# Residue-ordered keys, copied queries and negated scores in the dilated and windowed attention groups, with new durations for the planner

## The chip, the cores and the metric

One core of one Trainium2 chip runs the whole program. The metric is the device time of one execution in microseconds (us): 1769.04 us before, the median of three executions (1765.94, 1769.04, 1773.9). In this document PE is TensorE, DVE is VectorE, ACT is ScalarE, POOL is GpSimd, and SP is the engine that issues every DMA.

## The reference

The kernel computes one layer of a decoder trunk over 2048 tokens of width 1024. RMSNorm and one combined projection feed four groups of four heads; the merged heads are gated, projected by `w_out` and added to `x`:

```python
h = rms_norm(x, norm_w[layer]) @ w_in[layer]
o_a = dilated_attention(rms_norm(heads(a_q), g[0]), rms_norm(heads(a_k), g[1]), heads(a_v), tables[0])
o_b, _ = banded_attention(rms_norm(heads(b_q), g[2]), kb, vb, tables[1], SWA_WINDOW - 1, sink=attn_sinks[layer])
# group C: differential attention, group D: native sparse attention
y = jnp.concatenate([merge(o_a), merge(o_b), merge(o_c), merge(o_d)], axis=-1) * jax.nn.silu(silu_gate)
x = x + y @ w_out[layer]

DILATED_CONFIGS = ((128, 1), (512, 4), (2048, 16))
# dilated_attention: for each (window, rate) the tokens are folded into `rate` residue classes,
# banded_attention runs in each class over window // rate predecessors, and a softmax over the
# three log-sum-exps weighs the three outputs
# banded_attention: s = q k^T * 64**-0.5 + bias(dist * rate), invalid keys -1e30;
# m = max(s) (B: max with the sink); p = exp(s - m); o = p v / sum(p)
```

So a query block of 128 tokens of one residue class meets the 128 keys of its own block and, unless it is the first, the 128 of the block before it: 128 or 256 columns of scores. At rate 16 a class has one block, at rate 4 it has four, at rate 1 sixteen.

## The kernel before, in words

**Stages.** The projections of the groups run in the order C, D, A, B (`project`, one 512-column and one shorter accumulation for each of 16 row tiles and group). They are written as generators, "fillers", that hand PE work while attention waits. Attention runs group C, then D (window, compressed, selected), then A at rates 16 and 4 for each of its heads, then A at rate 1 in turns with B. The output projection (`out_proj`, matmuls on L2159) is the last filler: the half that needs C and D ("CD", reads `wb`) can run from the end of D on, the half that needs A and B ("AB", reads `keys`, `AQ`, `ow`) follows.

**What sets the order.** Nothing waits dynamically except on semaphores. While the program is built, a planner keeps an estimated clock for each engine (`T`), adds an estimated duration for each operation (`op("DVE", 72.0, e)`), and takes the next piece of PE work whose inputs should be there (`drive`, `fill_step`, `poll`, `defer`). The order in which instructions are written, on every engine and on SP's queue, comes from these estimates; a changed number can move instructions anywhere.

**Precision.** A float32 operand is split in a high and a low part of the type fp32r, each on its own rows; a score takes two matmuls (x = 0, 1) into one bank.

**Queries and keys.** `turn` in `project` transposes four 128-token tiles of normalised queries or keys (L741) into one bank; ACT and DVE scale and split them, and they are stored as [column of the head, token] in the DRAM tiles `TQ` and `TK`, tokens in natural order.

**A at rates 16 and 4** (`make_a`, `a_unit`): `ORDER` lists 32 units, for each head four of rate 16 and four of rate 4. `qk_load` brings one head's queries and keys into SBUF (`QK`; heads 0 and 2 lie in `wb`, heads 1 and 3 in `AQ` and `keys`). A unit has four blocks in two halves, in all eight score matmuls on L1646. A block of a residue class is addressed in place, with a step of `rate` elements, both as the weights and as the moving operand:

```python
return slice(c0, c0 + (n - 1) * r + 1, r)      # in cols(), used for Q and for K
```

At rate 16 all eight matmuls have 128 columns. At rate 4 two have 128 and six have 256; the first unit of rate 1 (contiguous operands, L1646 too) has the same eight.

After the matmuls DVE adds the bias and takes the maximum in one custom instruction for each block (L1651) followed by a read of its accumulator; a small instruction for each half (L1656) writes the negated maximum to column 65 of the output tile `AO`; ACT takes the exponential (L1662); PE transposes the weights (L393), ACT and DVE split them (L399, L403), PE multiplies by the values (L422), ACT evacuates (L371), PE transposes back (L435), and DVE sums the two halves (L439, or L442 on ACT and L444).

**Group B** does the same on L1948 to L1968, with a maximum against the sink (L1958) and a negation (L1959).

Of the kernel before, what the change touches and what calls it, by code (L numbers as in the profile page):

```python
# [22 lines left out]
NEG = -1e30  # L23
# [79 lines left out]
def tile_hybrid_heads(ctx, tc, a):  # L103
# [355 lines left out]
    expo = const.tile([128, 32], F32, name="expo")  # L459
# [8 lines left out]
    sink = const.tile([128, 4], F32, name="sink")  # L468
    nlam = const.tile([128, 1], F32, name="nlam")
# [38 lines left out]
    def small_constants(dl):  # L508
        V.tensor_scalar(gains[:, 0:1], gains[:, 0:1], 32.0 ** -0.5, None, op0=OP.mult)
        V.tensor_scalar(gains[:, 1:4], gains[:, 1:4], 0.125, None, op0=OP.mult)  # L510
# [6 lines left out]
        A.activation(ls[:, 2:4], ls[:, 0:2], AF.Exp)  # L517
        V.scalar_tensor_tensor(nlam, ls[:, 3:4], -0.2, ls[:, 2:3], op0=OP.add, op1=OP.subtract)


    def bias_vectors(bp):
# [4 lines left out]
        V.memset(tp[96:128, :], NEG)  # L526
# [65 lines left out]
    def weights(g, first=None):  # L592
# [21 lines left out]
        def split(i, rw, e):  # L614
# [4 lines left out]
            e = op("ACT", av(hi - lo, 1), e)  # L619
# [11 lines left out]
    def project(g, first=None):  # L631
# [26 lines left out]
        def evac_qk(t, ps, e, st, keep):  # L658
            run_chain()
            A.activation(st, ps, AF.Copy)  # L660
            e = op("ACT", av(512), e)
# [3 lines left out]
            e = op("ACT", av(nn), e)  # L665
# [5 lines left out]
            def two():  # L671
# [6 lines left out]
                e2 = op("DVE", 130.0)  # L678
                G.tensor_tensor(ss[:, :nh], ss[:, :nh], expo[:, :nh], op=OP.pow)  # L679
                e3 = op("POOL", 190.0 * nh + 100.0, e2)  # L680
# [55 lines left out]
        def turn(t3, j, gi, keep):  # L736
# [3 lines left out]
            for i in range(4):  # L740
                PE.transpose(ps[:, i * 128:(i + 1) * 128], keep[i][0][:, j * 128:(j + 1) * 128], ident)  # L741
# [194 lines left out]
    def row_steps(pool, store, qk, H, t, need, done):  # L936
# [5 lines left out]
        def chunk(ci, k0, n):  # L942
# [41 lines left out]
    def group_c():  # L984
      with tc.tile_pool(name="cs", bufs=1) as cs, tc.tile_pool(name="cw", bufs=2) as cw:
# [34 lines left out]
        def make(h, t0):  # L1020
# [66 lines left out]
            def close(ot):  # L1087
# [7 lines left out]
                def rest():  # L1095
                    for i in range(2):
                        A.activation(sq, O[:, i], AF.Square, accum_out=ss[:, i:i + 1])
                    e2 = op("ACT", 2 * av(64, 1), e)
# [4 lines left out]
                    e3 = op("POOL", 1966.0, e2)  # L1103
# [135 lines left out]
    def group_d():  # L1239
      with tc.tile_pool(name="dk", bufs=1) as dk:  # L1240
# [39 lines left out]
        def weigh(pool, ot, t, br, den, Y, first):  # L1280
# [5 lines left out]
            op("DVE", 557.0)  # L1286
# [8 lines left out]
        with tc.tile_pool(name="dq", bufs=1) as dq, tc.tile_pool(name="dw", bufs=2) as dw:  # L1295
# [19 lines left out]
            def win_unit(t):  # L1315
# [5 lines left out]
                def scores(h, c):  # L1321
# [51 lines left out]
        with tc.tile_pool(name="ds", bufs=1) as ds_:  # L1373
# [18 lines left out]
          with tc.tile_pool(name="dc", bufs=2) as dw:  # L1392
# [84 lines left out]
            def largest(t, n, selc, e):  # L1477
# [13 lines left out]
                e = op("DVE", 3412.0, e)  # L1491
# [84 lines left out]

    def qk_load(h, x):
# [5 lines left out]
        else:  # L1583
            c = slice((x - 2) // 2 * n, ((x - 2) // 2 + 1) * n)
            aready[h] = mv(raw(k)[x % 2::2, :, c], TK["A"][h * 64:h * 64 + 64, :, c])

# [29 lines left out]
    def group_ab():  # L1616
      with tc.tile_pool(name="aw", bufs=2) as aw, tc.tile_pool(name="as", bufs=1) as as_:
# [8 lines left out]


        def a_unit(r, q0, setup, room, need, source, stats, close):
# [5 lines left out]
            def scores(half):  # L1634
                qs, ks, H = source()
                if half == 0:
                    st["P"] = aw.tile([128, 4, 256], F32, name="ap", bufs=3)
                    st["mx"] = aw.tile([128, 4], F32, name="amx", bufs=4)
                P, mx, O = st["P"], st["mx"], stats()
# [17 lines left out]
                e = op("DVE", 72.0, e)  # L1657

                def weights():
                    for j in (2 * half, 2 * half + 1):  # L1660
                        n = 128 * (1 + prevs[j])
                        A.activation(P[:, j, :n], P[:, j, :n], AF.Exp, bias=O[:, j, 65:66], accum_out=O[:, j, 64:65])  # L1662
                        st["e"] = op("ACT", av(n, 2), e)
                    st["half"] = st.get("half", 0) + 1
                defer(e, weights)

# [22 lines left out]
        def make_a(n):  # L1689
# [8 lines left out]

            def setup():
                if h < 3 and 1 <= n % 8 <= 6:  # L1700
                    qk_load(h + 1, n % 8 - 1)
                if q0 == 0:
# [15 lines left out]
            def source():  # L1718
                Q, K = QK[h % 2]

                def cols(j, i0, n):
                    rho, i = divmod(q0 + j, nb)
                    c0 = rho + r * 128 * (i - i0)
                    return slice(c0, c0 + (n - 1) * r + 1, r)
                return (lambda j: Q[:, cols(j, 0, 128)]), (lambda x, j, p: K[:, x, cols(j, p, 128 * (1 + p))]), Hs[h, r]
# [62 lines left out]
            u = a_unit(r, q0, setup, room, lambda: max(at("s"), aready[h]), source,  # L1788
# [449 lines left out]
```

## Time and profile before

| | |
|---|---|
| median of three executions | 1769.04 us |
| the profiled execution's own time | 1773.27 us |
| its span, first to last instruction | 1771.5 us |
| granted PE clock, mean | 0.988 |
| PE busy | 1709.5 us (97%) |
| DVE, ACT, POOL busy | 76%, 61%, 39% |

The profile is one execution. A matmul's recorded end is modelled and matmuls overlap, so a busy PE can still do more in the same time: the distance between the starts of successive matmuls tells the pace, not the length of one. In the timeline, equal instructions that follow each other are merged into one row with their count.

### The profile page before, as it was taken

What the parts mean: (1) busy time and instruction counts of PE and PEld (TensorE: products, weight loads), DVE (VectorE), ACT (ScalarE), POOL (GpSimd) and SP (SyncE); (2) the same over time, 40 slices, a digit from 0 to 9 for tenths busy, and PEclk for the clock granted to TensorE, in tenths of its full rate; (3) what the DMA queues carried; (4) which work ended last, traced back from release to release, by engine and by line L of the source; (5) the groups of instructions that cost most, each with busy time, mean ns of one, the idle gap of its engine ahead of it and who ended that gap; (6) DMA issues with size and microseconds to landing.
All of it is one profiled execution on the core that took longest, in us unless ns stands there. A gap on an engine that the chain in (4) does not pass through costs nothing.

```text
span 1771.5 us, 31769 instructions
## 1 busy us (share of the span) xinstructions
PE 1709.5 (97%) x10035; PEld 1503.3 (85%) x10035; DVE 1338.3 (76%) x4072; ACT 1072.3 (61%) x2588; POOL 692.8 (39%) x841
## 2 busy tenths in 40 slices
PE   7999999999998999899999999999999999999999
PEld 5878878888887889788888889899979999789987
DVE  4446689898999998488747868888366876888873
ACT  4345466656776756467646656777356776576651
POOL 4567554544544554211255552222521112433331
PEclk9999999999999999899999999999999999999999
DMA  7763554444445424642367533232375778999986
GB/s 246 223 198 108 184 171 144 121 118 139 116 143 159 146 91 152 188 117 88 125 194 226 170 108 96 59 97 85 105 238 169 233 226 259 278 313 311 320 283 213
DMA packets 283480, 308.24 MB, mean 174 GB/s; under 512 B 80256, under 2 KB 201216, under 8 KB 282640
## 3 DMA queue, kind: packets, MB, share of 16 engines
q1 hardware_dynamic: 283312, 306.21, 55.8%
q8 instruction: 80, 1.31, 0.3%
q14 instruction: 88, 0.72, 0.1%
HBM read 219.47 MB, written 86.92 MB: 173 GB/s over the span
## 4 chain that ended last, share of the span: by engine, by line
PE 51%; DVE 3%; issue 1%; DMA 1%; ACT 1%; POOL 0%; SPq 0%; DVEq 0%; POOLq 0%
PE j L840 11%; PE j L2159 9%; PE o L422 9%; PE pt L393 8%; PE s L1646 4%; PE s L950 4%; PE pt L435 3%; PE s L1336 1%; PE pt L2123 1%; PE s L1948 1%; PE s L1435 1%; PE pt L741 0%; DVE pl L403 0%; PE j L1164 0%; DMA xt<-in_xt_dram 0%
## 5 line engine op out<-in xcount | busy, mean ns | idle before, releaser
L840 PE MATMUL j<-wb,xh 128*128 128x512 f32 (+2 forms) x2048 | 618.2, 382 | 18.8 <-DVE wb L622 9.6
L840 PEld LDWEIGHTS j<-wb,xh 128*128 128x128 f32 x2048 | 373.1, 190 | 67.4 <-DVE wb L622 14.5
L840 PE MATMUL j<-wb,xl 128*128 128x512 f32 (+2 forms) x1024 | 385.4, 376 | 0.6 <-POOL xl L577 0.6
L399 ACT ACTIVATE ph<-pt 128x512 fp32r<-128x512 f32 (+4 forms) x486 | 266.0, 575 | 123.5 <-PE pt L393 117.0
L403 DVE TENSOR_TENSOR pl<-pt,ph 128x512 fp32r<-128x512 f32 (+4 forms) x486 | 311.9, 658 | 38.1 <-ACT ph L399 37.2
L840 PEld LDWEIGHTS j<-wb,xl 128*128 128x128 f32 x1024 | 194.3, 190 | 25.7 <-POOL xl L577 1.2
L679 POOL TENSOR_TENSOR ss<-ss,expo 128x6 f32<-128x6 f32 (+2 forms) x64 | 117.4, 1835 | 169.2 <-DVE ss L677 155.3
L577 POOL TENSOR_TENSOR xl<-xt,xh 128x512 fp32r<-128x512 f32 x112 | 149.2, 1333 | 9.3
L371 ACT ACTIVATE ot<-o 128x512 f32<-128x512 f32 (+1 forms) x160 | 81.5, 509 | 106.4 <-PE o L422 105.9
L571 POOL TENSOR_SCALAR xh<-xt 128x512 fp32r<-128x512 f32 x128 | 84.6, 661 | 134.2 <-DMA xt<-in_xt_dram 65.5
L950 PE MATMUL s<-keys,Q 128*128 128x512 f32 (+3 forms) x320 | 113.6, 400 | 12.7 <-DVE mx L952 6.1
L2113 POOL TENSOR_TENSOR xt<-xt,sq 128x512 f32<-128x512 f32 x32 | 41.3, 1290 | 184.2 <-PE s L1646 66.2
L952 DVE CUSTOM_DVE_ANT_0 prow<-s,Hs 128x512 f32<-128x512 f32 (+3 forms) x160 | 95.1, 604 | 19.3 <-PE s L950 18.8
L1066 DVE SCALAR_TENSOR_TENSOR pa<-pb,ra,pa 128x1024 f32<-128x1024 f32 (+4 forms) x96 | 107.5, 1147 | 2.3
L660 ACT ACTIVATE stqk<-j 128x512 f32<-128x512 f32 x64 | 38.2, 597 | 113.5 <-PE j L840 111.0
L952 DVE CUSTOM_DVE_ANT_0 pa<-s,H 128x512 f32<-128x512 f32 (+3 forms) x160 | 93.8, 603 | 14.0 <-PE s L950 11.3
L952 DVE CUSTOM_DVE_ANT_0 pb<-s,H 128x512 f32<-128x512 f32 (+3 forms) x160 | 93.1, 603 | 7.2 <-PE s L950 6.5
L1662 ACT ACTIVATE ap<-ap,AO 128x128 f32<-128x128 f32 (+1 forms) x192 | 86.4, 456 | 17.7 <-DVE AO L1656 17.5
L1050 ACT ACTIVATE pa<-pa,nm 128x128 f32<-128x128 f32 (+7 forms) x64 | 76.9, 1202 | 31.5 <-DVE nm L958 31.0
L674 DVE TENSOR_REDUCE ss<-sq 128x6 f32<-128x384 f32 (+2 forms) x64 | 39.3, 614 | 69.9 <-ACT sq L664 69.9
L435 PE MATMUL pt<-ident,ot 128*128 128x128 f32 x512 | 85.0, 278 | 3.1 <-ACT ot L371 2.6
L1050 ACT ACTIVATE pb<-pb,nm 128x128 f32<-128x128 f32 (+7 forms) x64 | 76.8, 1200 | 16.5 <-DVE nm L958 16.3
(267 smaller groups left out, 4207.4 us busy)
## 6 DMA issues: line engine op xcount, KB each, us to landing
xt<-in_xt_dram SPq DMA_DIRECT2D x128, 256.0 KB, 3.3
xr<-in_x_dram SPq DMA_DIRECT2D x16, 512.0 KB, 5.4
Q<-tqC SPq DMA_DIRECT2D x64, 128.0 KB, 3.4
DQ<-tqD SPq DMA_DIRECT2D x16, 512.0 KB, 4.8
raw<-gate_d SPq DMA_DIRECT2D x32, 256.0 KB, 4.2
stqk<-in_x_dram SPq DMA_DIRECT2D x32, 256.0 KB, 4.8
acc_d<-stqk SPq DMA_DIRECT2D x32, 256.0 KB, 4.5
stqk<-acc_d SPq DMA_DIRECT2D x32, 256.0 KB, 4.5
```

Of the source, the lines that this page charges most:

```text
L393: PE.transpose(ps[:rows, x * 128:(x + 1) * 128], src(), ident)
L399: A.activation(ph[:rows, :n], ps[:rows, :n], AF.Copy)
L403: V.tensor_tensor(pl[:rows, :n], ps[:rows, :n], ph[:rows, :n], op=OP.subtract)
L422: PE.matmul(u["po"][:, c0:c0 + wd], lhsT=lhsT(), rhs=x[:rows, col:col + wd], start=u["k"] == 1, stop=u["k"] == total, skip_group_check=True)
L435: PE.transpose(ps[:, i * 128:(i + 1) * 128], ot[:, i * 128:(i + 1) * 128], ident)
L577: G.tensor_tensor(l, xt, h, op=OP.subtract)
L679: G.tensor_tensor(ss[:, :nh], ss[:, :nh], expo[:, :nh], op=OP.pow)
L840: PE.matmul(ps[:, :n], lhsT=xx[:, ks], rhs=W[k][ww][:, lo:hi], start=(k == 0 and i == 0), stop=(k == KT - 1 and i == 2))
L950: PE.matmul(ps[:, :n], lhsT=q(), rhs=k[:, k0:k0 + n], start=(i == 0), stop=(i == np_ - 1))
L952: V.tensor_tensor_reduce(st["row"][:, k0:k0 + n], ps[:, :n], rev(H, t * 128 + 127 - k0, n), 1.0, LOW, OP.add, OP.max, st["mx"][:, ci:ci + 1])
L1050: A.activation(row[:, :nk], row[:, :nk], AF.Exp, bias=nm, accum_out=den[:, i, m:m + 1])
L2159: PE.matmul(ps, lhsT=xx[:, ks], rhs=OW[half, (k, c)][ww], start=(x == 0 and k == 0 and i == 0), stop=(x == len(halves) - 1 and k == 3 and ...
```

## The change

- **Keys.** For group A the two key transposes of each four tiles write their bank in another order: within each tile of 128 tokens, first all tokens with residue 0 modulo 16, then residue 1, and so on, eight tokens each. `TK["A"]` and all loads keep their sizes; the order of the keys within a tile is new. The score matmuls read runs of eight neighbouring keys: one run of each of the 16 tiles at rate 16, four runs of each tile at rate 4, and at rate 1 all 16 runs of the one or two tiles.
- **Queries.** POOL copies the 512 queries of a unit into one of four contiguous places (`OW4`, two tiles that the output weights used later anyway); `gather_more` does it up to four units ahead, once the head's loads have come (`aloaded`).
- **Negative scores.** The query gains of A and B and their bias columns are negated, the mask's value is positive, the custom instruction takes the minimum and writes it directly where the exponential reads its bias; the exponential has a scale of -1. L1656 in A and L1959 in B are gone. Where the matmul's columns stand in another order, the custom instruction reads the bank through a rearranged view.
- **Durations.** Some fourteen numbers of the planner are other ones, in projections, C, D, B and the output.

```diff
@@ project.turn
-                PE.transpose(ps[:, i * 128:(i + 1) * 128], keep[i][0][:, j * 128:(j + 1) * 128], ident)
+                to = ps[:, i * 128:(i + 1) * 128]
+                if g == "A" and j >= 2:
+                    to = to.rearrange("p (r i) -> p i r", r=16)
+                PE.transpose(to, keep[i][0][:, j * 128:(j + 1) * 128], ident)
@@ small_constants, bias_vectors
-        V.tensor_scalar(gains[:, 1:4], gains[:, 1:4], 0.125, None, op0=OP.mult)
+        V.tensor_scalar(gains[:, 1:3], gains[:, 1:3], -0.125, None, op0=OP.mult)
+        V.tensor_scalar(gains[:, 3:4], gains[:, 3:4], 0.125, None, op0=OP.mult)
...
-        V.memset(tp[96:128, :], NEG)
+        V.memset(tp[96:128, 0:8], -NEG)
+        V.memset(tp[96:128, 8:16], NEG)
+        V.tensor_scalar(tb[0:96, 0:8], tb[0:96, 0:8], -1.0, None, op0=OP.mult)
@@ durations (two of some fourteen)
-                e3 = op("POOL", 190.0 * nh + 100.0, e2)
+                e3 = op("POOL", {16: 2900.0, 8: 1640.0, 6: 1305.0}[nh], e2)
...
-                e = op("DVE", 72.0, e)
+                e = op("DVE", 194.0, e)
@@ group_ab
+        OW4 = [as_.tile([128, 1024], F32R, name="ow%d" % i) for i in range(2)]
+        AC = {}
+        def gather_more():
+            while len(AC) < len(ORDER) and ORDER[len(AC)][0] in aloaded and free("AC", 4) < INF:
+                n = len(AC)
+                h, r, q0 = ORDER[n]
+                hd = alloc("AC", 4)
+                C = OW4[hd[1] % 4 // 2][:, hd[1] % 2 * 512:hd[1] % 2 * 512 + 512]
+                Q = QK[h % 2][0].rearrange("p (c r) -> p r c", r=r)
+                if r == 16:
+                    G.tensor_copy(C.rearrange("p (j c) -> p j c", j=4), Q[:, q0:q0 + 4])
+                else:
+                    G.tensor_copy(C, Q[:, q0 // 4])
+                AC[n] = (C, hd, op("POOL", 1150.0, max(aready[h], hd[2])))
@@ a_unit.scores
-                        e = op("PE", mm(n) if r == 1 else max(217.0, 0.92 * n)) + 60.0
+                        e = op("PE", mm(n)) + 60.0
...
-                    V.tensor_tensor_reduce(P[:, j, :n], ps[:, s0:s0 + n], rev(H, n - 1, n), 1.0, LOW,
-                                           OP.add, OP.max, mx[:, j:j + 1])
+                    fr = ps[:, s0:s0 + n] if r == 16 else ps[:, s0:s0 + n].rearrange("p (b u) -> p u b", b=16 // r)
+                    V.tensor_tensor_reduce(P[:, j, :n], fr, rev(H, n - 1, n), 1.0, -LOW,
+                                           OP.add, OP.min, O[:, j, 65:66])
...
-                two = slice(2 * half, 2 * half + 2)
-                V.tensor_scalar(O[:, two, 65], mx[:, two], -1.0, None, op0=OP.mult)
-                e = op("DVE", 72.0, e)
...
+                        A.activation(P[:, j, :n], P[:, j, :n], AF.Exp, bias=O[:, j, 65:66], scale=-1.0,
+                                     accum_out=O[:, j, 64:65])
@@ make_a
+            def scored():
+                release(AC[n][1], T["PE"] + 60.0)
+                defer(T["PE"] + 100.0, gather_more)
...
-                return (lambda j: Q[:, cols(j, 0, 128)]), (lambda x, j, p: K[:, x, cols(j, p, 128 * (1 + p))]), Hs[h, r]
+                K, C = QK[h % 2][1], AC[n][0]
+                if r == 16:
+                    K = K.rearrange("p x (t r c) -> p x r t c", t=16, r=16)
+                    ks = lambda x, j, p: K[:, x, q0 + j]
+                else:
+                    K = K.rearrange("p x (t s a c) -> p x a s t c", s=4, a=4, c=8)[:, :, q0 // 4]
+                    ks = lambda x, j, p: K[:, x, :, (j - p) * 4:(j + 1) * 4]
+                return (lambda j: C[:, j * 128:(j + 1) * 128]), ks, Hs[h, r]
@@ make_b.scores
-                V.tensor_tensor(nm[:, c], mx[:, c], sink[:, 2 * g:2 * g + 2], op=OP.max)
-                V.tensor_scalar(nm[:, c], nm[:, c], -1.0, None, op0=OP.mult)
-                e = op("DVE", 260.0, e)
+                V.tensor_tensor(nm[:, c], nm[:, c], nsink[:, 2 * g:2 * g + 2], op=OP.min)
+                e = op("DVE", 250.0, e)
```

How the written order moves, at three places. Line numbers of the changed kernel are higher: L1675 is L1646 of before, L1682 is L1651, L2199 is L2159, L2153 is L2113. On POOL, where A begins, before (L2113 multiplies gates into the merged heads for the output projection, L1761 merges two rates of a head):

```order
L448 TENSOR_TENSOR Os<-Os,dens 128x128
L1553 TENSOR_TENSOR Os<-Os,yps 128x128
L2113 TENSOR_TENSOR xt<-xt,sq 128x512 x2
L1761 TENSOR_TENSOR AO<-AO,mg 128x16x65 x2
L1763 TENSOR_TENSOR AO<-AO 128x16x65
```

and after, where `ow_17176` and `ow_17177` are the two tiles of `OW4`:

```order
L448 TENSOR_TENSOR Os<-Os,dens 128x128
L1562 TENSOR_TENSOR Os<-Os,yps 128x128
L1651 COPY ow_17176<-wb 128x512 x2
L1651 COPY ow_17177<-wb 128x512 x2
L1653 COPY ow_17176<-wb 128x512
L2153 TENSOR_TENSOR xt<-xt,sq 128x512
L1653 COPY ow_17176<-wb 128x512
L1653 COPY ow_17177<-wb 128x512 x2
L1651 COPY ow_17176<-AQ 128x512 x2
L2153 TENSOR_TENSOR xt<-xt,sq 128x512
```

Eight copies for each head stand on POOL's queue, the first five of them ahead of a gate product that waits for its own inputs. On PE, in the rate-4 units of head 0, before:

```order
L393 MATMUL pt<-ident,ap 128x128 x4
L1646 MATMUL s<-wb 128x128 x2
L1646 MATMUL s<-wb 128x256 x2
L435 MATMUL pt<-ident,ot 128x128 x4
L393 MATMUL pt<-ident,ap 128x128 x4
L1646 MATMUL s<-wb 128x256 x4
L1646 MATMUL s<-wb 128x128 x2
L1646 MATMUL s<-wb 128x256 x2
```

and after:

```order
L393 MATMUL pt<-ident,ap 128x128 x4
L1675 MATMUL s<-wb,ow_17176 128x128 x2
L1675 MATMUL s<-wb,ow_17176 128x256 x2
L435 MATMUL pt<-ident,ot 128x128 x4
L1675 MATMUL s<-wb,ow_17176 128x256 x4
L2199 MATMUL j<-wb,xh 128x512 x2
L2199 MATMUL j<-wb,xl 128x512
L1675 MATMUL s<-wb,ow_17177 128x128 x2
L1675 MATMUL s<-wb,ow_17177 128x256 x2
L393 MATMUL pt<-ident,ap 128x128 x4
L1675 MATMUL s<-wb,ow_17177 128x256 x4
```

The same score matmuls stand there, with matmuls of the output projection between them; from the first rate-16 to the last rate-4 score, 138 of these stand in the order where 90 stood. On DVE, the first half of the first rate-16 unit before (`ISA` is the custom instruction, then the read of its accumulator):

```order
L1651 ISA ap,amx<-s,AH_1080 128x128
L1651 ISA amx 128x1
L1651 ISA ap,amx<-s,AH_1080 128x128
L1651 ISA amx 128x1
L1656 TENSOR_SCALAR AO<-amx 128x2
```

and after:

```order
L1682 ISA ap,AO<-s,AH_1085 128x128
L1682 ISA AO 128x1
L1682 ISA ap,AO<-s,AH_1085 128x128
L1682 ISA AO 128x1
```

Five rows for a half become four.

## Rows read from the trace of the kernel before

**Rows 1.** the page: busy time, share of the span, instructions by engine
```profile
PE 1709.5 (97%) x10035; PEld 1503.3 (85%) x10035; DVE 1338.3 (76%) x4072; ACT 1072.3 (61%) x2588; POOL 692.8 (39%) x841
```

**Rows 2.** the page: the chain that ended last, by engine
```profile
PE 51%; DVE 3%; issue 1%; DMA 1%; ACT 1%; POOL 0%; SPq 0%; DVEq 0%; POOLq 0%
```

**Rows 3.** windows: us, busy PE, PEld, DVE, ACT, POOL, PE clock, DMA share, GB/s
```profile
400.00:600.00 200.00, 190.15 (x1090) 165.90 (x1090) 185.75 (x511) 135.17 (x295) 94.81 (x120) 0.98 0.47 140
...
1345.00:1495.00 150.00, 149.32 (x929) 141.81 (x928) 108.89 (x431) 102.28 (x354) 26.45 (x19) 1.00 0.77 238
1495.00:1600.00 105.00, 100.10 (x649) 88.39 (x648) 91.67 (x295) 69.97 (x212) 33.29 (x41) 0.98 0.91 284
1600.00:1700.00 100.00, 100.00 (x678) 90.41 (x677) 85.71 (x314) 70.79 (x216) 34.67 (x49) 1.00 1.02 315
1700.00:1772.00 72.00, 67.63 (x347) 56.10 (x346) 36.12 (x84) 19.14 (x48) 15.96 (x19) 0.99 0.71 229
```

**Rows 4.** lines by form, 1345 to 1495 us, PE: line, shapes, count, busy us, mean ns
```profile
L1646 PE MATMUL s<-wb 128*128 128x128 f32 x82 | 21.2, 396 | 0.0
...
L1646 PE MATMUL s<-wb 128*128 128x256 f32 x54 | 16.8, 438 | 0.0
...
L422 PE MATMUL o<-pl,tl 128*128 128x128 f32 x39 | 9.5, 276 | 0.2 <-DVE pl L403 0.2
...
L422 PE MATMUL o<-pl,tl 128*128 128x256 f32 x21 | 5.5, 282 | 0.0
```

**Rows 5.** the same view, weight loads
```profile
L1646 PEld LDWEIGHTS s<-wb 128*128 128x128 f32 x136 | 31.7, 311 | 0.2
...
L422 PEld LDWEIGHTS o<-pl,th 128*128 128x128 f32 x60 | 11.5, 192 | 0.2
```

**Rows 6.** timeline, PE: start us, us, merged instructions, three places
```profile
1367.47 2.23 PE L1646 MATMUL s<-wb 128*128 128x256 f32 x8
...
1380.26 0.95 PE L393 MATMUL pt<-ident,ap 128*128 128x128 f32 x7
...
1382.14 1.88 PE L1646 MATMUL s<-keys,AQ 128*128 128x128 f32 x8
...
1501.25 1.19 PE L1646 MATMUL s<-wb 128*128 128x128 f32 x8
```

**Rows 7.** lines by form, whole span, DVE: count, busy us, mean ns, idle before
```profile
L952 DVE CUSTOM_DVE_ANT_0 pa<-s,H 128x512 f32<-128x512 f32 x100 | 67.0, 683 | 8.5 <-PE s L950 7.8
...
L1651 DVE CUSTOM_DVE_ANT_0 ap<-s,wb 128x256 f32<-128x256 f32 x60 | 23.1, 419 | 4.0 <-PE s L1646 4.0
...
L439 DVE TENSOR_REDUCE AO<-pt 128x256 f32<-128x512 f32 x27 | 18.6, 687 | 15.6 <-PE pt L435 15.6
...
L780 DVE TENSOR_TENSOR raw<-pt,post 128x512 f32<-128x512 f32 x6 | 6.0, 1082 | 0.0
...
L1656 DVE TENSOR_SCALAR AO<-amx 128x2 f32<-128x2 f32 x96 | 25.1, 261 | 3.5
...
L1959 DVE TENSOR_SCALAR bnm<-bnm 128x2 f32<-128x2 f32 x32 | 5.4, 169 | 1.1
```

**Rows 8.** lines, whole span: POOL, and the transposes L741 on PE
```profile
L571 POOL TENSOR_SCALAR xh<-xt 128x512 fp32r<-128x512 f32 x128 | 84.6, 661 | 134.2 <-DMA xt<-in_xt_dram 65.5 <-PE j L840 30.9 <-PE j L1164 17.6
...
L2113 POOL TENSOR_TENSOR xt<-xt,sq 128x512 f32<-128x512 f32 x32 | 41.3, 1290 | 184.2 <-PE s L1646 66.2 <-DVE sq L2110 61.8 <-DMA tkB<-th 15.5
...
L741 PE MATMUL pt<-ident,stqk 128*128 128x128 f32 x240 | 35.7, 280 | 2.2 <-POOL stqk L683 1.4 <-DVE pl L403 0.7
...
L1761 POOL TENSOR_TENSOR AO<-AO,mg 128x1040 f32<-128x1040 f32 x8 | 15.7, 1984 | 50.4 <-DMA tl<-vvA 25.4 <-DMA xt<-yC 20.7 <-ACT mg L1758 4.2
```

**Rows 9.** waits in 1345 to 1495 us: who for whom, us, times, longest
```profile
DVE ap L1651 <- PE s L1646: 16.4, 26, 1.7
...
PE pt L435 <- DVE xl L2133: 0.5, 1, 0.5
```

More of the change, by code (lines that the diff above doesn't have):

```diff
@@ L618, in split @@
             A.activation(h[:, lo:hi], rw[:, :hi - lo], AF.Copy, scale=nw[:, k:k + 1])
-            e = op("ACT", av(hi - lo, 1), e)
+            e = op("ACT", av(hi - lo, 1) + 60.0, e)
             def low():
@@ L660, in evac_qk @@
             A.activation(st, ps, AF.Copy)
-            e = op("ACT", av(512), e)
+            e = op("ACT", av(512) + 150.0, e)
             hs = alloc("sq", 1)
@@ L664, in evac_qk @@
             A.activation(sq[:, :nn], st[:, :nn], AF.Square)
-            e = op("ACT", av(nn), e)
+            e = op("ACT", av(nn) + 60.0, e)
             if g == "D":
@@ L677, in two @@
                 V.tensor_scalar(ss[:, :nh], ss[:, :nh], 1.0 / dh, re[:, t:t + 1], op0=OP.mult, op1=OP.add)
-                e2 = op("DVE", 130.0)
+                e2 = op("DVE", 248.0)
                 G.tensor_tensor(ss[:, :nh], ss[:, :nh], expo[:, :nh], op=OP.pow)
-                e3 = op("POOL", 190.0 * nh + 100.0, e2)
+                e3 = op("POOL", {16: 2900.0, 8: 1640.0, 6: 1305.0}[nh], e2)
                 def three():
@@ L1097, in rest @@
                         A.activation(sq, O[:, i], AF.Square, accum_out=ss[:, i:i + 1])
-                    e2 = op("ACT", 2 * av(64, 1), e)
+                    e2 = op("ACT", 626.0, e)
                     G.tensor_scalar(ss, ss, 1.0 / 64, EPS, op0=OP.mult, op1=OP.add)
@@ L1102, in rest @@
                     G.tensor_tensor(O, O, subln.unsqueeze(1).broadcast_to([128, 2, 64]), op=OP.mult)
-                    e3 = op("POOL", 1966.0, e2)
+                    e3 = op("POOL", 2170.0, e2)
                     last.append(defer(e3 + (LATE if (h, t0) != (3, 14) else 0.0), lambda: mv(dv(y_d["C"])[:, t0:t0 + 2, h * 64:h * 64 + 64], O)))
@@ L1285, in weigh @@
             V.tensor_tensor(wt, wt, sg4[:, t, :, br], op=OP.mult)
-            op("DVE", 557.0)
+            op("DVE", 400.0)
             dst = Y.rearrange("p (h d) -> p h d", d=64)
@@ L1345, in scores @@
                         V.tensor_reduce(nm, st["mx"][:, h, :nch], AX.X, OP.max, negate=True)
-                        e = op("DVE", 72.0, e)
+                        e = op("DVE", 194.0, e)
                         def weights():
@@ L1490, in largest @@
                 V.tensor_scalar(ng, im, -1.5e30, NEG, op0=OP.is_gt, op1=OP.mult)
-                e = op("DVE", 3412.0, e)
+                e = op("DVE", 3000.0, e)
                 def turn_ng():
@@ L1624, in h_load, with a_unit @@
             Hs[h, r] = H
-        def a_unit(r, q0, setup, room, need, source, stats, close):
+        OW4 = [as_.tile([128, 1024], F32R, name="ow%d" % i) for i in range(2)]
[12 more added lines that the diff above has]
+                AC[n] = (C, hd, op("POOL", 1150.0, max(aready[h], hd[2])))
+        def a_unit(r, q0, setup, room, need, source, stats, close, scored=lambda: None):
             nb = 16 // r
@@ L1665, in scores @@
                 defer(e, weights)
+                if half:
+                    scored()
             jobs = []
@@ L1786, in room @@
                 return 0.0 if q0 else free("AO", 4)
-            u = a_unit(r, q0, setup, room, lambda: max(at("s"), aready[h]), source,
-                       lambda: tiles(res[h, r][0]), close)
+            u = a_unit(r, q0, setup, room, lambda: max(at("s"), aready[h], AC[n][2] if n in AC else INF), source,
+                       lambda: tiles(res[h, r][0]), close, scored)
             u["after"] = after
@@ L1852, in setup @@
                     parts += [QK[1][0][:, i * 1024:(i + 1) * 1024] for i in range(2)]
-                    parts += [as_.tile([128, 1024], F32R, name="ow%d" % i) for i in range(2)]
+                    parts += OW4
                     out_weights("AB", [(w[:, 0:512], w[:, 512:1024]) for w in parts])
@@ L1936, in scores @@
                     st["P"] = aw.tile([128, 4, 256], F32, name="ap", bufs=3).rearrange("p (i j) c -> p i j c", i=2)
-                    for x in ("mx", "nm", "den"):
+                    for x in ("nm", "den"):
                         st[x] = as_.tile([128, 4], F32, name="b" + x, bufs=5)
-                P, mx, nm, den = st["P"], st["mx"], st["nm"], st["den"]
+                P, nm, den = st["P"], st["nm"], st["den"]
                 t = t0 + i
@@ L2106, in gate @@
             A.activation(th, gt, AF.Tanh, scale=0.5)
-            e = op("ACT", av(512), max(e, hd[2]))
+            e = op("ACT", av(512) + 43.0, max(e, hd[2]))
             def rest():
```

30 lines of the change are left out of this document (16 added, 14 removed).

## The prediction

> **What bounds the kernel now.** I read the page's busy shares first: PE is busy for 97% of the span, 1709.5 of 1771.5 us, and the next engine, DVE, for 76% [rows 1]. The chain that ended last agrees: half of the span is on PE and no other engine has more than 3% [rows 2]. The second view is the table by stage [rows 3]. Group A at rates 16 and 4 runs between 1345 and 1495 us. There PE is busy for 149.3 of 150 us at full granted clock (1.00, the level of 2.4 GHz), DVE for 109, ACT for 102, POOL for 26, and the DMA share is 0.77. In the waits of that stretch the long ones are others waiting for PE, DVE for the scores 16.4 us, while PE's waits are at most half a microsecond [rows 9]. So PE's work in this stage is time, one for one, until something else takes over.
>
> The third view tells how much of that work is slow. In the groups by form a score matmul on L1646 lasts 396 ns at 128 columns and 438 ns at 256, while a product with the values, with contiguous operands, lasts 276 and 282 ns [rows 4]; its weight load lasts 311 ns against 192 [rows 5]. These lengths overlap, so for the pace I take the timeline, where a unit's eight score matmuls are one merged row [rows 6].
>
> **The change part by part.** *Score matmuls, rate 16.* Eight of 128 columns take 1.88 us [rows 6]. Seven contiguous transposes of the same size take 0.95 us; less the last one's length of 0.276 us, six steps take 0.674 us, 0.112 us each, so eight would take 0.95 + 0.112 = 1.06 us. The saving is 0.82 us for a unit, and with 16 units 13.1 us.
>
> *Score matmuls, rate 4.* Two of 128 and six of 256 columns take 2.23 us; the first rate-1 unit has the same eight with contiguous operands and takes 1.19 us [rows 6]. The saving is 1.04 us, with 16 units 16.6 us. Together 29.7 us. The modelled lengths would give (396 - 276) x 160 + (438 - 282) x 96 = 34.2 us [rows 4], which I keep as the far end. The first sum supposes that keys in runs of eight stream like contiguous ones. The queries become contiguous in any case. What a run of eight costs no row shows; the bounds are the contiguous pace and that of today. I take the contiguous one: today 256 columns at a step of four need 0.28 us at most (2.23 / 8), 1.1 ns a column, and 128 at a step of sixteen 0.235 us (1.88 / 8), 1.8 ns a column, so a column is cheaper the nearer its neighbour lies, and in a run it is next to it.
>
> The Trainium skill, Advanced Engine Details and Errata, section SBUF Cachelines, says that SBUF is read in lines of 16 bytes and that two hits on a line are enough for the full rate. A run of eight float32 keys has four hits on each of two lines, so the sum by the rule is that of the contiguous pace. No run here shows it yet, and the slow steps of 16 and 64 bytes, one hit to a line, agree with it.
>
> *Rate 1.* 120 matmuls of 256 columns, contiguous today, will hop between two tiles after every eight keys. I take nothing, for the same reason; the dear end is the second rival.
>
> *Key transposes.* 32 of the 240 transposes on L741 (two banks by four row groups by four tiles) now write their bank with a step of eight elements. The trace has no strided write by PE. The bounds are 0 and the extra of a strided operand, 0.82 / 8 = 0.10 us each, 3.3 us in all; I take the upper one, since PE with a 64-byte step is the nearest row. What they are hidden by is nothing: they stand on PE.
>
> The same page of the Trainium skill, section PSUM Cachelines, says that a non-contiguous access to PSUM slows matmuls significantly, and gives no duration. It speaks against the change here: by it the 3.3 us stand, without it the sum would be 3.3 us lower.
>
> *Copies of the queries.* 32 copies of 128x512 on POOL. The bounds are a contiguous pass over 512 columns, 661 ns, and a product of two, 1290 ns [rows 8]. At the upper end they are 41 us; with the 26.5 us that POOL has in the stage [rows 3] that is 68 of some 125 us. They run up to four units ahead, so PE's other units hide them; behind them on POOL's queue stand only gate products and merges, of which a merge's longest instruction is 1984 ns [rows 8]. I take 0.
>
> *Negated scores.* 96 instructions of 261 ns and 32 of 169 ns go from DVE, 25.1 and 5.4 us [rows 7]; 64 of the 96 are in the stage, 16.7 us. The rearranged reads of a bank, 108 of 256 columns, cost between nothing and 200 ns each: a sum over pairs 64 elements apart in a bank lasts 687 ns for 512 elements, as long as the custom instruction on contiguous ones, 683; the one row whose output is strided lasts 1082 [rows 7]. I take the first, for it too reads a bank. Even at 200 ns they are 21.6 us and DVE does less than before. PE hides all of it: 0.
>
> *Less cover in the stage.* With the 29.7 us gone the stage has 120 us for the same ACT work, 102 / 120 = 85%, where it was 68%. In 1600 to 1700 us, with DVE at 86% and ACT at 71%, PE waits for nothing; in 400 to 600 us, with DVE at 93%, it idles for 9.85 of 200 us, 4.9% [rows 3]. A value between, 3.3% of 120, is 4 us. The order puts 48 more matmuls of the output projection between the units, so the gaps have something to hold.
>
> *Durations.* They move fillers: before the 480th score matmul of the program stand 2196 matmuls of the projections where 2091 stood. PE's work is the same. Only its waits can change, 62 us in the whole program (1771.5 - 1709.5), in both directions: 0, with 10 us on either side.
>
> The sum against the profiled execution: 1773.3 - 29.7 + 3.3 + 4 = 1750.9 us. That execution is 4.2 us above the median of 1769.0, so I forecast 1747 us.
>
> **The rivals.** *DMA takes over.* From 1495 to 1700 us the share is 0.91 and 1.02 [rows 3]. From 1345 us on, DMA is busy for 0.77 x 150 + 0.91 x 105 + 1.02 x 100 + 0.71 x 72 = 364 of 427 us. With 26 us less that is 0.91 on the mean. If 0.91, that of the stretch in which PE idles 4.9 us of 105, were all that holds until the last 72 us, those 313 us would take 344 and the rest 72: 416, a saving of 11 us, and with the transposes 1761 us. For it: transfers come in bursts. Against it: 1.02 was held for 100 us without a wait of PE.
>
> *Short runs are slow.* If keys in runs of eight stream at the pace of the 64-byte step, 0.235 us for 128 columns, rate 16 saves nothing, a rate-4 unit needs 2 x 0.235 + 6 x 0.47 = 3.29 us, 1.06 more than now (17 us in all), and rate 1 pays (0.47 - 0.149) x 120 = 38.5 us, 0.149 being 1.19 / 8. With the transposes the time is 1828 us, slower. At the pace of rate 4, 0.28 us for 256 columns, rate 16 saves (0.235 - 0.14) x 128 = 12.2 us, rate 4 saves (2.23 - 1.96) x 16 = 4.3, rate 1 pays 15.7, the transposes 3.3: 1772 us. So it decides from about 1.1 ns a column. Against it: the pace improves with nearness, as said.
>
> *The moved fillers cost.* Projection work drawn forward is missing later: before the 928th score matmul 2883 stand where 2835 did, so 48 fewer are left to cover what remains of the selection stage. Uncovered, they are 48 x 0.21 us (a start distance of 512 columns at 2.4 GHz) or 10 us: 1757 us. For it: 400 to 600 us shows that covered attention still idles. Against it: the same move fills earlier waits.
>
> **How the numbers follow.** Forecast 0.72, DMA 0.12, short runs 0.08 (half at either pace), fillers 0.08. The forecast's own range is 1735 to 1756: 4.5 us more saved by the lengths, no price for the transposes and no new idle time make 12 us below; twice the idle time and some order make 9 above. The order's 10 us take the low end to 1728; DMA and fillers together take the high end to 1766. What a measurement can tell is 0.5%, 8.8 us: faster means under 1760.2. To faster go 0.70 of the forecast, 0.05 of DMA and 0.04 of the fillers, 0.79. Slower gets the slow half of the short runs, 0.04, and 0.03 of the others, 0.07; 0.14 is left for the same.
>
> **What would show it.** In the profile after, a unit's eight score matmuls should take about 1.06 us at rate 16 and 1.2 at rates 4 and 1; weight loads of the scores should last about 190 ns; the transposes with the strided write more than 280 ns if the price is right. The stage of rates 16 and 4 should be some 28 us shorter for the same work, with ACT its busiest engine after PE, and the DMA share near 0.9. The prediction is wrong if rate 1's row grows beyond 1.3 us, if PE waits for a DMA or for POOL's copies by more than 5 us in all, or if the stages before 1345 us change by more than 10 us.

## The result: slower, and the profile after

The changed kernel takes 1817.0 us in the median of four runs (1815.0 to 1824.8) against 1770.4 us for the kernel before beside it: a ratio of 1.028, with a 95% interval of 1.0258 to 1.0302. I had forecast 1747 us and a range up to 1766, so even the sign was wrong.

The page shows that PE has less to do and takes longer. First its busy line, after: engine, busy us, share of the span, instructions. PE did 1709.5 us in 97% of the span before [rows 1].

```profile
PE 1698.2 (94%) x10035; PEld 1491.2 (82%) x10035; DVE 1310.4 (72%) x3948; ACT 1066.5 (59%) x2579; POOL 725.5 (40%) x873
```

Then the chain that ended last, after, by engine. DMA had 1% of it [rows 2] and has 5% now.

```profile
PE 42%; DMA 5%; DVE 4%; ACT 1%; issue 1%; POOL 1%; SPq 1%; POOLq 0%; DVEq 0%; ACTq 0%
```

The windows of the kernel after tell where (columns as in [rows 3]: length, busy PE, PEld, DVE, ACT, POOL, granted clock, DMA share, GB/s).

```profile
1345.00:1495.00 150.00, 149.13 (x1093) 137.73 (x1092) 115.02 (x418) 117.70 (x402) 60.21 (x49) 0.99 0.89 287
1495.00:1600.00 105.00, 86.11 (x497) 74.20 (x496) 69.19 (x203) 48.57 (x146) 33.29 (x42) 0.90 0.81 249
1600.00:1700.00 100.00, 75.56 (x463) 67.04 (x461) 56.88 (x190) 49.09 (x150) 21.30 (x31) 0.88 0.73 217
1700.00:1814.00 114.00, 93.53 (x512) 80.25 (x512) 56.20 (x170) 41.01 (x118) 23.98 (x33) 0.89 0.59 188
```

Between 1345 and 1495 us PE now does 1093 matmuls where it did 929: the stage that was to gain has gained. From 1600 to 1700 us it does 463 where it did 678, busy for 75.56 us at a granted clock of 0.88 where it was busy for all 100 at 1.00. The DMA share fell as well, from 1.02 to 0.73, so DMA has not taken over either.

Four sections sum up the difference of the two spans. They are read off the first and last start of the score line (L1646 before, L1675 after). Rate 1 has 128 score matmuls, in both kernels the last 128 that read `wb` (duration min/median/max in ns, first and last start in us; before, then after):

```profile
L1646 PE MATMUL s<-wb x128: 225/282/365, 1491.1 to 1701.6; 128*128 128x256 f32 x120, 128*128 128x128 f32 x8
L1675 PE MATMUL s<-wb x128: 220/294/579, 1467.4 to 1752.7; 128*128 128x256 f32 x120, 128*128 128x128 f32 x8
```

| section | before, us | after, us | difference |
|---|---|---|---|
| start to the first score of group A | 1350.2 | 1342.3 | -7.9 |
| to the first rate-1 score | 140.8 | 125.1 | -15.7 |
| to the last rate-1 score | 210.6 | 285.3 | +74.7 |
| to the end | 69.9 | 61.2 | -8.7 |

The scores themselves are not what got slow. In the groups by form of the kernel after, 1345 to 1495 us, a score matmul takes 280 to 308 ns, where it took 396 and 438 [rows 4] (line, shapes, count, busy us, mean ns, idle before).

```profile
L1675 PE MATMUL s<-keys,ow 128*128 128x128 f32 x80 | 12.5, 280 | 0.0
L1675 PE MATMUL s<-wb,ow 128*128 128x128 f32 x72 | 11.5, 292 | 0.0
...
L1675 PE MATMUL s<-wb,ow 128*128 128x256 f32 x48 | 8.9, 308 | 0.0
L1675 PE MATMUL s<-keys,ow 128*128 128x256 f32 x48 | 8.2, 301 | 0.0
```

The waits of PE after 1495 us say what it lacks, after: who for whom, us, times, longest.

```profile
PE s L1675 <- DMA wb<-tkA: 36.3, 7, 7.7
PE s L1675 <- DMA out_dram<-stqk: 11.3, 1, 11.3
PE o L422 <- DVE pl L403: 3.8, 2, 3.3
PE s L1675 <- DMA wb<-vvA: 2.3, 1, 2.3
```

The scores of rate 1 wait for their keys' load. A piece of the chain of the kernel after, 1560 to 1700 us, shows the rhythm (start us, us, what; the 55 longest pieces).

```profile
1566.74 6.20 DMA wb<-tkA
1572.98 2.08 PE s L1675 x8
1575.06 1.28 PE j L2199 x3
...
1583.46 5.28 DMA wb<-tkA
1588.73 1.00 issue
1589.73 1.22 PE s L1675 x8
```

A load of 5 to 6 us ends, the scores start at once, and the next load is issued only 10 to 17 us later. The timeline after shows more. At 1638 us a load goes out between the two halves of a unit's scores, four matmuls each, and the second half waits for it (start us, us, engine, what; in brackets PE's idle time before the row and what ended it).

```profile
1636.15 0.74 PE L1675 MATMUL s<-wb 128*128 128x256 f32 x4
1638.48 1.20 SPq L156 DMA_DIRECT2D wb<-tkA  x2
1645.38 1.19 PE L1675 MATMUL s<-wb 128*128 128x256 f32 x4 [7.57 <-DMA wb<-tkA]
```

Before, a load went out 8 to 11 us ahead of the scores that come next, so its 6 us lay beside other work, as the timeline of the kernel before shows.

```profile
1640.53 1.17 SPq L156 DMA_DIRECT2D wb<-tkA  x2
1650.20 1.02 PEld L1646 LDWEIGHTS s<-wb 128*128 128x128 f32 x8
1650.32 1.11 PE L1646 MATMUL s<-wb 128*128 128x256 f32 x8
```

There are two buffers for the keys in both kernels; after, they work like one.

### The profile page after: what moved, and what is told of

It reads as the page before. It is cut to its first block, busy times and chain, and to the rows that moved or that the text cites. A ratio compares the mean times of both kernels' runs of the same rounds, so it can differ in the third digit from the quotient of the medians.

```text
span 1813.9 us, 31755 instructions
## 1 busy us (share of the span) xinstructions
PE 1698.2 (94%) x10035; PEld 1491.2 (82%) x10035; DVE 1310.4 (72%) x3948; ACT 1066.5 (59%) x2579; POOL 725.5 (40%) x873
## 4 chain that ended last, share of the span: by engine, by line
PE 42%; DMA 5%; DVE 4%; ACT 1%; issue 1%; POOL 1%; SPq 1%; POOLq 0%; DVEq 0%; ACTq 0%
PE j L849 9%; PE j L2199 8%; PE o L422 7%; PE pt L393 6%; PE s L959 3%; PE s L1675 3%; DMA wb<-tkA 2%; PE pt L435 2%; PE s L1345 1%; PE s L1989 1%; PE pt L2163 1%; DMA raw<-gate_d 1%; DMA BK<-tkB 1%; SPq L156 1%; PE s L1444 1%
## 5 line engine op out<-in xcount | busy, mean ns | idle before, releaser
L583 POOL TENSOR_TENSOR xl<-xt,xh 128x512 fp32r<-128x512 f32 x112 | 150.7, 1345 | 9.3
L577 POOL TENSOR_SCALAR xh<-xt 128x512 fp32r<-128x512 f32 x128 | 88.7, 693 | 101.8 <-DMA xt<-in_xt_dram 77.1
L961 DVE CUSTOM_DVE_ANT_0 pa<-s,H 128x512 f32<-128x512 f32 (+3 forms) x160 | 94.2, 605 | 12.6 <-PE s L959 9.9
L1075 DVE SCALAR_TENSOR_TENSOR pa<-pb,ra,pa 128x1024 f32<-128x1024 f32 (+4 forms) x96 | 99.6, 1064 | 2.3
L2153 POOL TENSOR_TENSOR xt<-xt,sq 128x512 f32<-128x512 f32 x32 | 41.2, 1287 | 149.7 <-DVE sq L2150 53.0
```

Source lines behind the costliest of these rows:

```text
L583: G.tensor_tensor(l, xt, h, op=OP.subtract)
L961: V.tensor_tensor_reduce(st["row"][:, k0:k0 + n], ps[:, :n], rev(H, t * 128 + 127 - k0, n), 1.0, LOW, OP.add, OP.max, st["mx"][:, ci:ci + 1])
```

## The experiments

All were timed in three rounds beside the kernel before.

**First batch: is it the order, or the operations?** I began with the theory that the new order issues the rate-1 loads too late, and with the durations as a rival. *old_durations* is the changed kernel with the twelve durations outside groups A and B set back:

```
-            e = op("ACT", av(hi - lo, 1) + 60.0, e)
+            e = op("ACT", av(hi - lo, 1), e)
 ... and eleven more
```

> The changed kernel with the dozen durations of projections, C, D and the output set back; keys by residue, copied queries and negated scores stay. Theory 'no slack' (the order written for rate 1 and B gives the loads of a rate-1 unit no reserve; one delay turns into a chain of waits through SP's queue): depends on where this order puts those loads, between 1745 and 1800 us; the rate-16/4 stage is about 124 us in any case. Theory 'durations' (the new numbers wrote a bad order): about 1745 us. Theory 'operations' (the reordered keys, rearranged reads or copies are slow themselves in the rate-1 stage): about 1815 us.

Measured: 1806.1 us, ratio 1.0201 (1.0172 to 1.0229).

*durations_only* is the kernel before with these twelve alone.

> The kernel before with only the dozen durations changed. Theory 'no slack': near 1770 us, within 15 either way, as the rate-16/4 stage keeps its length. Theory 'durations': 1800 us or more, with waits for the loads of rate-1 units. Theory 'operations': 1770 us.

Measured: 1772.2 us, 1.0013 (0.9998 to 1.0027). The durations alone are no cause.

*after_lead4* tells the planner that rate 1's loads land 4 us later than it thinks:

```
-            a1ready[m] = mv(raw(Va[:, :n]), ...)
+            a1ready[m] = mv(raw(Va[:, :n]), ...) + 4000.0
```

> The changed kernel, but the planner takes the loads of each rate-1 unit as there 4 us later, so that it puts more filler before the unit's scores. Nothing that runs is added. Theory 'no slack': waits of PE for the loads of rate-1 units fall from 36 us to under 10, granted clock from 1500 to 1750 us back to 0.98 or more, and 1750 to 1770 us in all. Theories 'operations' and 'durations': 1805 us or more.

Measured: 1827.2 us, 1.0314 (1.0285 to 1.0344), and PE waits 41.0 us for wb<-tkA. More room in the plan didn't help.

*before_order* has every operation of the change, but all the planner's durations as before, so that the order is that of the kernel before but for POOL's copies.

> All operations of the change, but every duration of the planner as before, those of group A's and B's scores too: the order of before, but for POOL's copies. Theory 'no slack': 1740 to 1760 us, as the order of before has a reserve of 2 to 3 us for the loads and the rate-16/4 stage is shorter. Theory 'operations': 1800 us or more. Theory 'durations': 1745 us.

Measured: 1823.9 us, 1.0299 (1.0274 to 1.0324). Its wait of PE:

```profile
PE s L1675 <- DMA wb<-tkA: 44.0, 9, 8.4
```

Under the old order the wait is as long. My first theory fell, and the rival with it: some operation of the change brings the wait, wherever the order puts it.

**What the scores really wait for.** Next I followed the semaphores of the compiled program, to see which instruction each wait stands for. Each rate-1 unit has two halves, and before, it waits once for its loads, in the first half. After, this stands there (instruction numbers of an engine, columns of the tile wb):

```
PE score 9614  reads keys from 11136, first half of a unit   waits for SP load 1899, its own queries (10624)
PE score 9628  reads keys from 11392, second half            waits for SP load 1933, keys of the NEXT unit, written to 8704
SP load 1933   writes columns 8704 to 9983                    waits for PE score 9617, the last of that first half
```

The 1280 columns from 8704 and the 1280 from 11136 are two buffers and have nothing in common. Yet the second half waits for the load, and the load for the first half. The new view of the keys, `K[:, x].rearrange("p (t b c) -> p b t c", b=16, c=8)`, sliced by tile, has three free dimensions (16, 2 and 8 elements); the old slice had one. Both buffers lie in the one tile `wb`. So the theory became: with this view the dependency tracking takes a read to touch the other buffer too; each load has to stand between scores that read the other buffer, and double buffering is lost. (Whether the number of dimensions or the strides of the view bring this about, no run separates.) The rival was that the strided and copied operands are slower in some way that the rows don't show.

**Second batch.** *own_tiles* keeps every instruction of the change at its place and moves only addresses: the rate-1 keys get a tile of their own with two buffers, and group B's keys and queries their room in wb.

```
-            K = wb[:, base + 512:base + 1792].rearrange("p (i c) -> p i c", i=2)
+            K = as_.tile([128, 2, 640], F32R, name="AK1", bufs=2)
...
-            Kb = as_.tile([128, 2, 384], F32R, name="BK", bufs=2)
+            at_ = 8192 + len(Bs) % 2 * 2432 + 512
+            Kb = wb[:, at_:at_ + 768].rearrange("p (i c) -> p i c", i=2)
 ... and Qb behind it
```

> The whole change, every instruction and its place as there, only other addresses: the two rate-1 key buffers get a tile of their own (AK1, two buffers), and the key and query buffers of group B take their room in wb. In the changed kernel the second half of a rate-1 unit's scores waits for the key load of the next unit, which goes to the other buffer: a false dependency, since the view of the keys with three free dimensions is taken to reach over all of wb. Theory 'false wait': with the keys in their own tiles no score waits for the next unit's load and no key load for another unit's scores, the 36.3 us that PE's L1675 waits for wb<-tkA fall under 8, the granted clock of 1500 to 1700 goes back from 0.86 to 0.93 to 0.98 or more, and the time is 1747 (1735 to 1765), which is what I had forecast. Rival 'operations': the strided views, the copies and the negated scores themselves cost it; then the time stays at 1800 to 1825.

Measured: 1758.3 us, 0.9923 (0.9901 to 0.9946). 59 us are back for a change of addresses. PE's waits on its keys, in own_tiles:

```profile
PE s L1675 <- DMA AK<-tkA: 4.7, 2, 3.6
```

*contig_r1* removes the view instead of the shared tile: the matmul reads the keys as they lie, and writes its scores into PSUM in runs of eight.

```
-   ks: K[:, x].rearrange("p (t b c) -> p b t c", b=16, c=8)[:, :, q0 + j - p - lo:q0 + j + 1 - lo]
+   ks: K[:, x, (q0 + j - p - lo) * 128:(q0 + j + 1 - lo) * 128]
+   to = ps[:, s0:s0 + n].rearrange("p (b t c) -> p t b c", b=16, c=8)      (rate 1, written by PE.matmul)
```

> The whole change but for rate 1's reading of its keys: the matmul takes them as they lie (one free dimension, so no wait on the other buffer), and writes its scores into PSUM in runs of 8 at a stride, in the order in which VectorE then reads them. Theory 'false wait': 1747 (1735 to 1770), a few us over own_tiles if the strided write has a price (rate 1's x8 rows, 1.13 us in the changed kernel, tell that). Rival 'operations': 1800 to 1825.

Measured: 1755.2 us, 0.9919 (0.9888 to 0.9950). The wait for wb<-tkA is 3.5 us, once.

*before_view* does the reverse, and puts the view alone into the kernel before:

```
-   ks: K[:, x, (q0 + j - p - lo) * 128:(q0 + j + 1 - lo) * 128]
+   ks: K[:, x].rearrange("p (t b c) -> p b t c", b=16, c=8)[:, :, q0 + j - p - lo:q0 + j + 1 - lo]
+   to = ps[:, s0:s0 + n].rearrange("p (t b c) -> p b t c", b=16, c=8)
```

> The kernel before with only rate 1's keys read through a view of three free dimensions inside wb (each tile's columns by 8 at a stride of 8 times 16, written back to their places in PSUM): nothing of the change's order, copies, negation or durations. Theory 'false wait': the same waits appear in the kernel before, PE waits 20 us or more for wb<-tkA, the granted clock of its rate-1 stage (1500 to 1700) falls from 0.96 or more to under 0.93, and the time is 1800 to 1840 (1817 less 1747 is 70 us, on a kernel without the faster rates 16 and 4, less what its order hides). Rival 'operations': 1765 to 1780.

Measured: 1840.4 us, 1.0391 (1.0366 to 1.0416): 70 us for one view, and the write that undoes its order, in a kernel that has nothing else of the change. PE's largest wait, and its windows:

```profile
PE s L1649 <- DMA wb<-tkA: 43.2, 8, 9.4
```

```profile
1495.00:1600.00 105.00, 88.80 (x543) 78.47 (x543) 77.69 (x245) 56.73 (x171) 28.87 (x35) 0.92 0.84 259
1600.00:1700.00 100.00, 77.68 (x463) 69.16 (x462) 60.61 (x219) 49.61 (x153) 23.43 (x35) 0.86 0.72 216
```

In 1600 to 1700 us PE does the same 463 matmuls as after the change, at nearly the same clock. Since contig_r1 writes PSUM in the same runs of eight and is fast, it isn't that write. The false wait is shown from both sides: taken away in two ways, and brought in alone.

*own_tiles_old* is own_tiles with the twelve durations set back.

> own_tiles with the dozen durations outside groups A and B as before. Theory 'false wait': within 10 us of own_tiles, since those durations alone made the kernel before 1.0013 times as long; 1738 to 1757. Rival 'durations cost 11 us' (1817.0 against 1806.1 with the old ones, both with the false wait): 1736, 11 us below own_tiles.

Measured: 1744.3 us, 0.9853 (0.9829 to 0.9876), the fastest version of all. It is 14 us below own_tiles, not within 10; the rival's 11 us was nearer. That it lies within 3 us of my forecast is in part luck: it is not the change as made, and the 7.3 us that the sum took for transposes and lost cover did not show. From its first to its last rate-1 score PE works at the pace of the kernel before again, 1315 matmuls in 203 us against 1370 in 211 (windows of own_tiles_old, then of before):

```profile
1476.80:1679.60 202.80, 197.18 (x1315) 176.95 (x1314) 166.12 (x554) 140.56 (x431) 67.78 (x90) 0.97 0.97 302
1491.00:1701.60 210.60, 205.70 (x1370) 184.21 (x1369) 182.78 (x628) 146.06 (x444) 69.33 (x91) 0.99 0.96 300
```

**Third batch: controls, and the durations again.** *before_own* moves the same addresses in the kernel before (the diff of own_tiles).

> The kernel before with only the move of the rate-1 keys into a tile of their own and of group B's keys and queries into wb: a control, since the kernel before reads its keys through views with one free dimension. Theory 'false wait': nothing to free, 1770 (1764 to 1776). Rival 'the new addresses themselves are faster': below 1760, and then own_tiles (1758.3) would say little.

Measured: 1768.8 us, 0.9997 (0.9985 to 1.0010). The addresses alone are worth nothing.

*neg_only* has only the negated scores, with the planner's numbers that belong to them:

```
-                    V.tensor_tensor_reduce(P[:, j, :n], ps[...], rev(H, n - 1, n), 1.0, LOW,  OP.add, OP.max, mx[:, j:j + 1])
+                    V.tensor_tensor_reduce(P[:, j, :n], ps[...], rev(H, n - 1, n), 1.0, -LOW, OP.add, OP.min, O[:, j, 65:66])
-                V.tensor_scalar(O[:, two, 65], mx[:, two], -1.0, None, op0=OP.mult)
 ... and the sign in gains, bias table and exponential, and group B
```

> The kernel before with only the negated scores of groups A and B (the sign in the gains of A and B, in the bias table and in the exponential; minimum for maximum; 32 instructions of VectorE of about 0.07 to 0.26 us by the planner's costs gone a stage). My term for it was 0: 1770 (1764 to 1776). Rival: VectorE's small instructions stand between a score and its exponential and PE waits for them (16.4 us for ap in [rows 9]); then 1760 or less.

Measured: 1767.9 us, 0.9999 (0.9987 to 1.0011). Removing 128 instructions of VectorE gives nothing.

*own_tiles_p* and *own_tiles_s* are own_tiles with the first five (projections) or the last seven (groups C, D, gate) of the twelve durations set back.

> own_tiles with the five durations of the projections (scaled weights, the two of the query and key evacuation, mean square, power) as before, the seven of groups C, D and the gate as changed. Own_tiles took 1758.3 and with all twelve as before 1744.3. Theory 'one part does it': 1744 here and 1758 in own_tiles_s, or the other way round. Rival 'any other order of the fillers moves the time by some us': both between, 1745 to 1757.

> own_tiles with the seven durations of groups C, D and the gate as before, the five of the projections as changed. Theory 'one part does it': 1744 here if own_tiles_p is at 1758, and 1758 if that is at 1744. Rival 'any other order of the fillers': both between, 1745 to 1757.

Measured: 1759.7 us, 0.9952 (0.9936 to 0.9969), and 1767.2 us, 0.9990 (0.9974 to 1.0005). Neither half gives the 14 us between own_tiles and own_tiles_old back, and the second lies above both. So no one part does it, nor do the parts add up; that both would lie between was wrong too.

## Why the prediction was wrong

*The step that failed* is "Rate 1. [...] I take nothing": the sum has no term for a wait that the new view brings. I asked only how fast the matmul would stream its keys, and that was answered nearly rightly: a rate-1 unit's eight scores, where they don't stand behind a load, take 1.13 to 1.33 us (timeline after; one row below), where they took 1.10 to 1.20 ([rows 6] has one of 1.19).

```profile
1520.06 1.13 PE L1675 MATMUL s<-wb 128*128 128x128 f32 x8
```

I didn't ask what the new view does to the order that the semaphores enforce. The price is about 60 to 70 us however measured: 1817.0 less own_tiles' 1758.3 is 59, less contig_r1's 1755.2 is 62, with the old durations 1806.1 less 1744.3 is 62, and before_view less before is 70. What it consists of is read from after and own_tiles, which give PE the same work from the first to the last rate-1 score (windows after, then of own_tiles):

```profile
1467.40:1752.70 285.30, 228.54 (x1378) 201.41 (x1377) 175.27 (x564) 144.97 (x440) 66.58 (x90) 0.89 0.75 228
1468.10:1694.60 226.50, 213.95 (x1379) 188.78 (x1378) 173.08 (x564) 144.76 (x440) 66.71 (x90) 0.98 0.93 288
```

Of the 59 us between them, 44 are idle time (56.8 against 12.6), and 15 are busy time: the same matmuls take longer at a mean granted clock of 0.89 than at 0.98. The row of 2.08 us in the chain above stands right behind a wait of 7.7 us, and from 1572.9 to 1575.1 us the granted clock was 0.50, the level of 1.2 GHz.

None of my rivals was it. DMA did not take over, as its share fell, and the stages before group A got 8 us shorter, so the moved fillers did not cost there. "Short runs are slow" gave 1828 us, near the time measured, and for a wrong reason: the rows deny its mechanism, and own_tiles, with the same short runs, is fast. That a rival's number fits is no evidence for it. Two signs that I had named did appear: "PE waits for a DMA [...] by more than 5 us in all", and rows of rate 1 "beyond 1.3 us". The second is no sign of slow runs here: the rows of 1.8 to 2.1 us all stand behind waits, and of the others only one passes 1.3, with 1.33. One sum was off without effect: the range's low end of 1735 less 10 is 1725, not 1728.

*Scores at rates 16 and 4* were right. A unit's eight matmuls at rate 16 take 1.00 to 1.09 us (forecast 1.06) and at rate 4 1.14 to 1.25 (forecast 1.2), leaving out the first two, of 2.0 and 1.8 us: PE had waited 3.4 us for the first copy, and from 1342 to 1345 and 1345 to 1348.5 us the granted clock was 0.50 and 0.57. Two rows of the timeline after, one of each rate:

```profile
1401.38 1.01 PE L1675 MATMUL s<-wb,ow 128*128 128x128 f32 x8
```

```profile
1461.81 1.25 PE L1675 MATMUL s<-keys,ow 128*128 128x128 f32 x8
```

Weight loads last 191 and 201 ns against 311 [rows 5]. The stage between the first score and the first rate-1 score is only 15.7 us shorter (12 in own_tiles_old), but more of the output projection stands in it, 138 matmuls for 92 (147 in own_tiles_old; lines by form from 1350.2 to 1491.0 us before, from 1342.3 to 1467.4 us after):

```profile
L2159 PE MATMUL j<-wb,xh 128*128 128x512 f32 x61 | 19.6, 402 | 0.0
L2159 PE MATMUL j<-wb,xl 128*128 128x512 f32 x31 | 12.2, 393 | 0.0
L2199 PE MATMUL j<-wb,xh 128*128 128x512 f32 x92 | 31.1, 420 | 0.0
L2199 PE MATMUL j<-wb,xl 128*128 128x512 f32 x46 | 18.4, 400 | 0.0
```

Nine of them in a row take 2.07 us in the chain after, 0.23 each, so by this estimate the 46 are 10.6 us of work drawn forward, and for the same work the stage is some 26 us shorter, where the forecast's signs said some 28. So runs of eight float32 stream like contiguous columns here. By the Trainium skill, Advanced Engine Details and Errata, section SBUF Cachelines, they should, and these rows agree.

*Less cover*: 4 us taken, none found in the stage. PE is busy for 124.6 of its 125.1 us (windows after). ACT is its busiest engine after PE and the DMA share is 0.90, as forecast, but ACT is at 77%, not 85%:

```profile
1342.30:1467.40 125.10, 124.56 (x924) 116.07 (x925) 94.28 (x359) 96.41 (x339) 61.13 (x49) 0.98 0.90 289
```

*Key transposes*: 3.3 us taken, none found. The groups by line of the kernel after show 35.7 us for the 240 transposes, as before [rows 8].

```profile
L750 PE MATMUL pt<-ident,stqk 128*128 128x128 f32 x240 | 35.7, 280 | 2.0 <-POOL stqk L689 1.9
```

The same page of the Trainium skill, section PSUM Cachelines, speaks of a significant slowdown for a non-contiguous PSUM access. Here the strided write of 32 transposes in 240 leaves their mean at 280 ns and their sum at 35.7 us, and the scores of contig_r1, written in runs of eight, last no longer than others (median 282 ns against 287 in own_tiles); the measurement decides.

*Copies of the queries*: taken at 0. They last 1.08 to 1.17 us each, inside my bounds, and PE waits for them 3.4 us, once, at the first unit, behind which the clock was low as said.

```profile
L1653 POOL CAST ow<-wb 128x512 fp32r<-128x512 f32 x8 | 9.4, 1174 | 7.0 <-PE s L1675 7.0
L1651 POOL CAST ow<-AQ 128x512 fp32r<-128x512 f32 x8 | 9.0, 1156 | 3.4 <-PE s L1675 3.4
```

*Negated scores*: 0, as neg_only shows. The rearranged read of PSUM by DVE costs nothing: 420 ns for 256 columns where it was 419 [rows 7].

```profile
L1682 DVE CUSTOM_DVE_ANT_0 ap<-s,wb 128x256 f32<-128x256 f32 x60 | 22.7, 420 | 56.5 <-PE s L1675 56.5
```

*Durations*: 0 with 10 us on either side, and the size was off. Alone they do nothing (1.0013), but with the rest of the change they cost 11 us with the false wait (1817.0 less 1806.1) and 14 without it. The trace of own_tiles puts it in the rate-1 stretch, 226 us long against 203 in own_tiles_old (first to last score), though it begins 9 us earlier, and its chain there runs over the load queue:

```profile
1663.49 4.66 DMA yA<-AO
1669.10 3.12 DMA raw<-gate_d
1672.31 0.63 ACT sq L2147
1672.94 0.99 ACT ap L2006 x4
1673.93 0.60 SPq L156
1674.59 1.42 SPq L156
1676.06 0.54 SPq L156
1676.64 5.99 DMA wb<-tkB
1682.77 2.05 PE s L1990 x8
```

A store of yA holds the queue until it has landed: the next issue on it is the load of yA into xt at 1668.21 us, and the next units' keys stand behind both. SP waits for yA 11.3 us in 1500 to 1700 us, 11.9 in own_tiles_p, 11.2 in own_tiles_s and 10.5 in contig_r1, and not at all in own_tiles_old and before. So the wait stands in the versions that lost and not in the fastest, but no run changed it alone: that it is the cause is not shown, and which duration sets that order stays open.

## What to carry to other kernels

When an edit changes an access pattern, look at its waits as well as its pace: list which instruction each semaphore wait stands for, before and after, above all where several buffers are cut out of one large tile. Give double buffers tiles of their own, or read them through a view of one free dimension; both brought the time back here. If PE waits for a load that was issued late, ask first what held the issue back; here neither more room in the plan nor the old order could cure it, and an address did.

## What was unexpected

A matmul that reads 16 x 2 x 8 elements at columns 11392 on waited for a load to columns 8704 to 9983 of the same tile: the dependency is one of the program, not of the chip, and cost 60 to 70 us. Of the hardware itself, the granted clock of PE was 0.86 to 0.92 in the stretches in which PE waited for loads (before_view, 1495 to 1700 us), and 0.98 to 1.00 in the same stretches of the kernel before [rows 3]; so the stall cost more than its own length, in after against own_tiles 15 us beside 44 of idle time.
